# The gate of an encoder layer: from eight to seven block products, its weights prepared during the MLP, its sigmoid from one ScalarE function

## The chip, the cores and the metric

The kernel runs on one core of a Trainium2 chip. The core has five engines with queues of their own: TensorE (PE in the profile, with its weight loads as PEld), VectorE (DVE), ScalarE (ACT), GpSimd (POOL) and SyncE (SP), which here issues nearly all transfers. The metric is the device time of one execution in microseconds (us); less is better.

## The reference

One layer of an encoder runs over 1280 tokens (1024 and 256) of width 1024: an attention half, an MLP of width 4096 with squared ReLU, and then the part that is changed here, in 32-bit floats:

```python
gate = sigmoid(rms_norm(h, g_ple) @ w_ple_gate)      # (T, 1024) x (1024, 1024)
h = h + gate * (p @ w_ple_proj)                      # (T, 256) x (256, 1024)
y = rms_norm(h, g_final)
```

`rms_norm(h, g)` divides each row by the root of its mean square (plus 1e-6) and multiplies by the gains g.

## The kernel before

Every product of 32-bit operands is made from three products of a fast format: an operand a is split into a high part ah (a rounding copy on ScalarE) and a low part al = a - ah (a subtraction on VectorE or GpSimd), and PE adds ah·bh, ah·bl and al·bh into one PSUM bank (`split3`, L156 and L264). One matmul is 128x128 stationary by up to 512 moving columns.

The two MLP products are done as block products after Winograd's form of Strassen's scheme: both operands are cut into 2x2 blocks, and seven products of sums of blocks stand for the usual eight. The second MLP product goes through 56 steps m, eight for each of seven block products in the order O2 = 1, 7, 6, 4, 5, 3, 2. In step m `put2(m)` issues 30 matmuls, `prep(m + 3)` splits the operands of three steps later (a copy of 1280 columns and one of 1024 on ScalarE, L1384 and L1385, the same again as subtractions on VectorE, L1386 and L1387), and at its end `load2(m + 5)` asks for the operands of five steps later over SP's queue: 640 KB of activations from DRAM (`ar`) and none, one or two pieces of 512 KB of weights (`w2r`). The operand buffers rotate over three, so `prep(m + 3)` waits until `put2(m)` has been read. After a block's eighth step `evac2` adds the five PSUM banks to the residual h, which lies in four quadrants of 5 tiles x 512 columns (`hq`, by token half and column half).

The gate before is a plain product. From step 32 on `gate_w` loads rows of w_gate, multiplies them by g_ple and splits them, so that all eight 128-row pieces lie in SBUF; `gate_input(t)` transposes one token tile of h on PE (8 transposes, L1517), splits it (L1518, L1519) and makes the row scale rn = 1/rms from a squared sum, Ln and Exp with one correcting step (`rsqrt`, L138 to L144). Ten token tiles t then follow one another. For each of two column halves there are 24 gate matmuls (`psg`, L1588) and 6 of the embedding's product (`psp`, L156); the sigmoid is computed as exp(-ln(1 + exp(-z))) with a correction: ScalarE L1592, VectorE L1593, ScalarE L1594 and L1595, GpSimd L1596, VectorE L1597. The result multiplies the embedding (L1613), is added to h (GpSimd, L1615), is squared for the final norm (ScalarE, L1616), and VectorE applies row scale and gain (L1644) before the store. The last tile is cut into pieces of 512, 256 and 256 columns, and its arithmetic is on VectorE in place of GpSimd.

The order of the work on each engine comes from a scheduler that runs while the program is built: it walks the program with a simulated clock and gives each engine its instructions in that order; `issue_after(x)` forces what is in its block to come after x on x's engine. Each engine then works through its own queue in order. Tiles of one `slot` share one buffer, so a new tile waits until the last user of the old one is through.

Of the kernel before, what the change touches and what calls it, by code (L numbers as in the profile page):

```python
# [16 lines left out]
F16 = mybir.dt.float16  # L17
AF = mybir.ActivationFunctionType
# [5 lines left out]
P = 128  # L24
# [21 lines left out]
def encoder_kernel(ctx: ExitStack, tc: tile.TileContext, x, xT, pT, w_in, w_out, w_ff1, w_ff2, w_gate, w_proj,  # L46
# [88 lines left out]
    def rsqrt(dst, src, scale, eps, tp, n, tag):  # L135
        vv = tp.tile([P, n], F32, tag=f"{tag}v", name=f"{tag}v")
        uu = tp.tile([P, n], F32, tag=f"{tag}u", name=f"{tag}u")
        V.tensor_scalar(vv, src, scale, eps, op0=ALU.mult, op1=ALU.add)  # L138
        S.activation(uu, vv, AF.Ln)
        S.activation(dst, uu, AF.Exp, scale=-0.5)  # L140
        if n == 1:
            S.activation(uu, dst, AF.Copy, scale=-0.5)
            V.scalar_tensor_tensor(vv, dst, dst, vv, op0=ALU.mult, op1=ALU.mult)
            V.scalar_tensor_tensor(dst, vv, -3.0, uu, op0=ALU.add, op1=ALU.mult)  # L144
            return
# [3 lines left out]
        V.tensor_tensor(dst, dst, uu, op=ALU.mult)  # L149

# [57 lines left out]
    def open_slots(pool_, tags):  # L208
        for tag in tags:
            slot_pool[tag] = pool_  # L210
            size = {"H": 2560, "L": 2560, "W": 1024, "Q": 1280, "K": 1280, "T": 512}[tag[0]]
            slot(tag, [P, size], F32, tag)
# [1128 lines left out]
    open_slots(fq, ["Q2", "Q3"])  # L1341
# [8 lines left out]
    AOS, WOS, ARS, WRS = ("H0", "H2", "H3"), ("H1", "L7", "L5"), ("L1", "L6"), ("W8", "W9", "Q0", "Q1", "Q2", "Q3")  # L1350
# [3 lines left out]
    kt2 = {}  # L1354
    wr_n = itertools.count()
    w2v = w_ff2.rearrange("(b c x r) n -> b x r c n", c=2, x=2, r=P)

    def load2(m):
# [3 lines left out]
        t = AR[m] = slot(ARS[m % 2], [P, 2, HT], F32, "ar")  # L1362
        dma(t, ad[i][b].rearrange("c p t -> p c t"))
        WR[m] = []
        for x, y in WSRC[i]:
            if i == 1:
                t = kt2[b] = slot(KTS[b], [P, 2, 512], F32, "kt2")
            else:
                t = slot(WRS[next(wr_n) % 6], [P, 2, 512], F32, "w2r")
                WR[m].append(t[:])  # L1370
            dma(t, w2v[b, x][:, :, y * 512:y * 512 + 512])

    def prep(m):
# [13 lines left out]
        V.tensor_tensor(wo[:, 1], w, f(wo[:, 0]), op=ALU.subtract)  # L1387
# [13 lines left out]
    def load_h(half, n, tag):  # L1401
# [4 lines left out]
    BANKS = ("f2 pj f1 f2 tr", "pj tr f1 f2 pj", "f2 tr f1 pj tr", "f2 pj f1 f2 tr", "tr pj f1 f2 pj",  # L1406
             "f1 f2 tr tr pj", "f1 f2 pj f1 f2")
# [68 lines left out]
    FORD = [TORD[2 * j + h] for h in (1, 0) for j in range(HP)]  # L1476
    gw, pw, n3 = [], [], {}
    g_n = itertools.count()

    def w_raw(src):  # L1480
        n = next(g_n)
        t = slot("W10" if n < 4 else f"W{8 + n % 2}", [P, D], F32, "graw")
        dma(t, src)
        return t

    def gate_w(k, tags):
        raw = w_raw(w_gate[k * P:(k + 1) * P, :])
        if len(tags) == 1:
            t = at32(tags[0], [P, 2, D], F32R, "gw")
            a, b = t[:, 0], t[:, 1]  # L1490
        else:
            a, b = (slot(t, [P, D], F32R, "gw")[:] for t in tags)
        S.activation(a, raw, AF.Copy, scale=gple[:, k:k + 1])
        V.scalar_tensor_tensor(b, raw, gple[:, k:k + 1], f(a), op0=ALU.mult, op1=ALU.subtract)
        gw.append((a, b))

    def proj_w(k, tag):
        raw = w_raw(w_proj[k * P:(k + 1) * P, :])
        t = at32(tag, [P, 2, D], F32R, "pw")
        S.activation(t[:, 0], raw, AF.Copy)  # L1500
        V.tensor_tensor(t[:, 1], raw, f(t[:, 0]), op=ALU.subtract)
        pw.append((t[:, 0], t[:, 1]))

    gi_n = itertools.count()

    def h_half(t, n):
        j, half = divmod(TORD.index(t), 2)
        return h_of(j, half, n)

    def gate_input(t):  # L1510

        n3_ = at32(("H5", "L4")[next(gi_n) % 2], [P, 2, KD, P], F32R, "n3")
        n3h, n3l = n3_[:, 0], n3_[:, 1]
        for n in range(2):
            tr = pp2[0].tile([P, 4, P], F32, tag="tr", name="trg", bufs=2)
            for k in range(4):
                PE.transpose(tr[:, k], h_half(t, n)[:, k * P:(k + 1) * P], ident)  # L1517
            S.activation(n3h[:, 4 * n:4 * n + 4], tr, AF.Copy)  # L1518
            V.tensor_tensor(n3l[:, 4 * n:4 * n + 4], tr, f(n3h[:, 4 * n:4 * n + 4]), op=ALU.subtract)  # L1519
        ss = gq_.tile([P, 2], F32, tag="gss", name="gss")  # L1520
        for n in range(2):
            jk = gq_.tile([P, 512], F32, tag="gjk", name="gjk", bufs=1)
            S.activation(jk, h_half(t, n), AF.Square, accum_out=ss[:, n:n + 1])
        V.tensor_tensor(ss[:, 0:1], ss[:, 0:1], ss[:, 1:2], op=ALU.add)
        rn = gq_.tile([P, 1], F32, tag="grn", name="grn")
        rsqrt(rn, ss[:, 0:1], 1.0 / D, 1e-6, gq_, 1, "grs")
        S.activation(rn, rn, AF.Copy, scale=-1.0)
        return n3h, n3l, rn

    QUADS = {2: (0, 0, "H6"), 3: (0, 1, "L2"), 4: (1, 0, "H4"), 5: (1, 1, "L3")}  # L1530
    for m in range(NM):
# [3 lines left out]
        if m + 3 < NM:  # L1535
            prep(m + 3)

        if m >= 4 * NB and m % 4 == 0 and len(gw) < 4:
            gate_w(len(gw), KTS[2 * len(gw):2 * len(gw) + 2])
        if m == NM - 4:  # L1540
            fqs.close()
            gq_ = pool("gq", side="left", bufs=2)
            gq_.tile([P, 8], F32, name="gpad", bufs=1)
            for k in range(2):
                gate_w(4 + k, (ARS[k],))
        elif m == NM - 3:
            gate_w(6, (AOS[m % 3],))
            gate_w(7, (WOS[m % 3],))
            n3[FORD[0]] = gate_input(FORD[0])
# [147 lines left out]
```

## Time and profile before

| | us |
|---|---|
| median of 3 runs | 1693.11 (1692.22 to 1693.23) |
| profiled execution | 1691.84 |
| its span in the profile | 1690.1 |
| PE busy | 1651.6 |
| DVE busy | 1179.9 |
| ACT busy | 868.0 |
| POOL busy | 661.0 |
| the seven block products of the second MLP product | 1152 to 1535 |
| the gate, from its first matmul to the last of all | 1535 to 1679 |

The page of the profile lists busy time by engine, the span in 40 slices, the DMA queues, the chain of work that ended last, and the costliest groups of instructions; other views give the same for a stretch of time, for one line, or in order of time. "x24" is a count, and "<- PE" after an idle time names what ended it.

### The profile page before, as it was taken

The numbers are of one execution on the slowest core, as the hardware profiler recorded it, in microseconds if no ns is written. First come the engines' busy times: TensorE is split into PE (matmuls) and PEld (weight loads), VectorE is DVE, ScalarE is ACT, GpSimd is POOL, SyncE is SP. The second block draws the span as 40 slices with busy tenths as digits, with TensorE's granted clock in tenths as the row PEclk, the third lists the DMA queues.
The fourth block names the chain that finished last, engine by engine and source line by source line (L and its number), as shares of the span: only waits on it lengthen the run. The fifth ranks groups of instructions, "written<-read, shape, count | busy, mean of one in ns | idle before, by whom it ended". The sixth has DMA issues, their size and how long they took to land.

```text
span 1690.1 us, 27269 instructions
## 1 busy us (share of the span) xinstructions
PE 1651.6 (98%) x9849; PEld 1482.7 (88%) x9849; DVE 1179.9 (70%) x2119; ACT 868.0 (51%) x1749; POOL 661.0 (39%) x647
## 2 busy tenths in 40 slices
PE   8999999999899999999999999999999999999997
PEld 8999888888788888889999999998888888888886
DVE  7778588777888888668666666666665855445666
ACT  8643377776766667674333333233433333354554
POOL 1223455555654445433566665620532400001441
PEclk9999999999999999999999999999999999999999
DMA  9766843433954524395443343349676356532111
GB/s 309 239 216 237 247 144 110 133 108 98 273 161 130 154 74 131 108 330 172 160 136 131 132 159 128 135 169 386 220 225 203 124 192 210 177 117 75 35 44 50
DMA packets 191867, 278.28 MB, mean 165 GB/s; under 512 B 13674, under 2 KB 121076, under 8 KB 191732
## 3 DMA queue, kind: packets, MB, share of 16 engines
q1 hardware_dynamic: 189988, 271.28, 49.7%
q0 software_dynamic: 1600, 5.24, 1.0%
q8 instruction: 78, 1.28, 0.3%
q14 instruction: 57, 0.47, 0.1%
q10 hardware_dynamic: 144, 0.00, 0.0%
HBM read 182.63 MB, written 88.61 MB: 160 GB/s over the span
## 4 chain that ended last, share of the span: by engine, by line
PE 79%; DVE 8%; ACT 4%; issue 4%; POOL 2%; DMA 2%; POOLq 0%; SPq 0%; ACTq 0%; DVEq 0%
PE psa L264 6%; PE sc L651 6%; PE av L729 5%; PE psb L264 4%; PE pso L264 4%; PE tr L705 4%; PE psv L264 2%; PE psg L1588 1%; DVE pl L716 1%; DVE p L686 1%; DMA xt<-in_x 1%; POOL hq L1615 1%; DMA xr<-in_xT 1%; PE f__15605 L156 1%; PE f__16642 L156 1%
## 5 line engine op out<-in xcount | busy, mean ns | idle before, releaser
L1384 ACT ACTIVATE ao<-ar 128x1280 fp32r<-128x1280 f32 x56 | 71.2, 1273 | 183.7 <-PE f__15946 L156 36.6
L651 PE MATMUL sc<-kt,qt 128*128 128x512 f32 (+1 forms) x576 | 156.6, 392 | 8.8 <-ACT p L676 6.1
L716 DVE TENSOR_TENSOR pl<-tr,ph 128x512 fp32r<-128x512 f32 x204 | 138.0, 685 | 32.0 <-ACT ph L711 30.8
L1386 DVE TENSOR_TENSOR ao<-ar,ao 128x1280 fp32r<-128x1280 f32 x56 | 93.3, 1666 | 85.2 <-ACT ao L1384 85.2
L711 ACT ACTIVATE ph<-tr 128x512 fp32r<-128x512 f32 x204 | 120.0, 596 | 59.2 <-PE tr L705 52.7
L651 PEld LDWEIGHTS sc<-kt,qt 128*128 128x128 f32 x576 | 98.8, 189 | 27.1 <-ACT p L676 7.6
L264 PE MATMUL pso<-ow,mt 128*128 128x512 f32 x480 | 119.9, 396 | 2.0 <-DVE osq L756 1.3
L705 PE MATMUL tr<-ident,p 128*128 128x128 f32 x768 | 116.0, 274 | 5.8 <-DVE pl L716 5.1
L1588 PE MATMUL psg<-gw,n 128*128 128x512 f32 (+1 forms) x504 | 113.7, 381 | 0.0
L705 PEld LDWEIGHTS tr<-ident,p 128*128 128x128 f32 x768 | 91.6, 141 | 22.6 <-DVE pl L716 9.0
L1105 POOL TENSOR_SCALAR w1r<-w1r,gmlp 128x256 f32<-128x256 f32 x112 | 80.3, 735 | 68.4 <-DMA w1r<-in_w_ff 68.4
L1588 PEld LDWEIGHTS psg<-gw,n 128*128 128x128 f32 x504 | 90.9, 188 | 17.8
L264 PEld LDWEIGHTS pso<-ow,mt 128*128 128x128 f32 x480 | 88.0, 189 | 19.9 <-DVE osq L756 2.0
L729 PE MATMUL av<-ph,vt 128*128 128x256 f32 x544 | 101.8, 288 | 1.0 <-ACT ph L711 0.4
L690 POOL TENSOR_SCALAR p<-p,rl 128x1024 f32<-128x1024 f32 x64 | 76.2, 1192 | 50.6 <-DVE rl L688 49.1
L1178 ACT ACTIVATE w<-w1s 128x512 fp32r<-128x512 f32 x56 | 35.2, 629 | 114.7 <-POOL w1s L1185 55.3
L668 DVE TENSOR_REDUCE mm<-sc 128x1 f32<-128x1024 f32 (+1 forms) x80 | 84.2, 1056 | 9.4 <-PE sc L651 9.0
L729 PE MATMUL av<-pl,vt 128*128 128x256 f32 x408 | 89.4, 300 | 0.0
L729 PEld LDWEIGHTS av<-ph,vt 128*128 128x128 f32 x544 | 81.8, 188 | 6.4 <-DVE osq L756 0.8
L676 ACT ACTIVATE p<-sc,mm 128x1024 f32<-128x1024 f32 x64 | 71.4, 1116 | 25.1 <-DVE mm L668 16.3
L664 DVE CUSTOM_DVE_ANT_0 p<-sc,dist 128x1024 f32<-128x1024 f32 x64 | 77.6, 1218 | 7.8 <-PE sc L651 3.8
L673 ACT ACTIVATE p<-p,mm 128x1024 f32<-128x1024 f32 x64 | 73.5, 1149 | 18.0 <-DVE mm L664 17.2
(1520 smaller groups left out, 4705.9 us busy)
## 6 DMA issues: line engine op xcount, KB each, us to landing
ar<-ad SPq DMA_DIRECT2D x56, 640.0 KB, 4.0
w2r<-in_w_ff SPq DMA_DIRECT2D x56, 512.0 KB, 4.6
qt<-qd SPq DMA_DIRECT2D x160, 128.0 KB, 3.0
ad<-q SPq DMA_DIRECT2D x64, 320.0 KB, 2.8
ad<-qs SPq DMA_DIRECT2D x48, 320.0 KB, 2.2
w1r<-in_w_ff SPq DMA_DIRECT2D x28, 512.0 KB, 4.3
md<-ml SPq DMA_DIRECT2D x40, 256.0 KB, 2.5
mt<-md SPq DMA_DIRECT2D x20, 512.0 KB, 5.7
```

Source lines behind the costliest of these rows:

```text
L264: PE.matmul(ps, a, b, start=i == 0, stop=i == n - 1)
L651: PE.matmul(ps[:, h0:h0 + n], shared["q"][:, cc, v, i * P:(i + 1) * P], kt[:, s0 + h0:s0 + h0 + n], start=v == 0, stop=v == 1)
L664: V.tensor_tensor_reduce(out=p[:, :sn], in0=ps[:, :sn], in1=dst_t[:, off:off + sn], scale=SLOPES[idx], scalar=3.0e38, op0=ALU.add, op1=ALU ...
L668: V.tensor_reduce(out=st["m", i][:, 0:1], in_=ps[:, :sn], axis=AX.X, op=ALU.max, negate=True)
L690: G.tensor_scalar(p[:, :sn], p[:, :sn], rl[:, 0:1], 1.0, op0=ALU.mult, op1=ALU.mult)
L705: PE.transpose(t[:, jj, i * P:(i + 1) * P], st["ws"][i][:, j * P:(j + 1) * P], ident)
L711: S.activation(ph, st["tr", j2], AF.Copy)
L716: V.tensor_tensor(pl, st["tr", j2], f(st["ph", j2][:]), op=ALU.subtract)
L729: PE.matmul(st["av"][:, :256], x_, y_, start=j2 == 0 and n == 0, stop=j2 == nj - 1 and n == len(pr) - 1)
L1105: G.tensor_scalar(raw[:, k], raw[:, k], gmlp[:, 4 * kh + k:4 * kh + k + 1], 1.0, op0=ALU.mult, op1=ALU.mult)
L1386: V.tensor_tensor(ao[:, 1], a, f(ao[:, 0]), op=ALU.subtract)
L1588: ends[:] = [PE.matmul(ps, a, b, start=m == 0, stop=m == len(pr) - 1)]
```

## The change

The gate's product is done with the same seven block products (ORDER 1, 2, 6, 5, 3, 7, 4) on the quadrants of h and of g_ple·w_gate. Each has 5 token tiles x 4 x 3 matmuls. Sums of products are kept in two SBUF buffers m1 and u3; the products 2, 3, 7 and 4 finish one quadrant of the gate each, and only these have the embedding's product, the sigmoid and the addition to h (`gate_half`).

- **Weights.** In steps 29 to 43 of the MLP, a generator `gate_operands` takes one step after each `prep`: two loads of four quarters of w_gate scaled on ScalarE, five block operands each (sums on VectorE, none on GpSimd), split through one staging buffer (L6) and written to DRAM (`bed`); the last three steps split the embedding's input pT and write it too (`ped`). `b_ops` loads a block operand back one block ahead. Those of blocks 2 and 3 are raw quarters, loaded and split in place.
- **Tokens.** `quad_tr` transposes a quadrant when the MLP has finished it: quadrants 12, 11 and 21 in the MLP's last 24 steps, 22 in the gate's first block. `a_op` splits a block operand of tokens one block ahead; their sums are on GpSimd.
- **Sigmoid.** One ScalarE function with the row scale as its scale. This function is in another ScalarE table than Ln and Exp; the table of these is loaded again near the end.
- **Row scales.** `rsqrt_d` starts from an integer estimate of 1/sqrt and takes three Newton steps, on VectorE for the gate and on GpSimd for most final norms; the last two tiles of the output keep Ln and Exp.
- **Last tile.** Two pieces of 256 columns; the final scaling is split over VectorE and ScalarE, and the last store is issued by ScalarE.
- **Around it.** The two `ar` buffers lie in one slot, which frees L6; three instead of six `w2r` buffers from step 40 on; PSUM banks of the MLP's blocks five and six are renamed, which frees two for the transposes.

```diff
+    def rsqrt_d(dst, ss, tp, n, tag, eng=V, bufs=None, rest=None):
...
+        eng.tensor_scalar(vv, ss, -0.5 / D, c, op0=ALU.mult, op1=ALU.add)
+        eng.tensor_scalar(dst.bitcast(I32), vv[:].bitcast(I32), -0.5, float(0x5F3759DF - 2**30 - 2**22), op0=ALU.mult, op1=ALU.add)
+        for _ in range(3):
+            if n == 1:
+                eng.tensor_scalar(uu, dst, dst, vv, op0=ALU.mult, op1=ALU.mult)
+                eng.tensor_scalar(dst, uu, 1.5, dst, op0=ALU.add, op1=ALU.mult)
...
-        t = AR[m] = slot(ARS[m % 2], [P, 2, HT], F32, "ar")
-        dma(t, ad[i][b].rearrange("c p t -> p c t"))
+        if m == 0:
+            AR["both"] = slot("L1", [P, 2, 2, HT], F32, "ar")
+        t = AR[m] = AR["both"][:, m % 2]
+        fetched[:] = [dma(t, ad[i][b].rearrange("c p t -> p c t"))]
...
+    def a_op(i, j, src, eng=V):
...
+        S.activation(t[:, 0], src, AF.Copy)
+        eng.tensor_tensor(t[:, 1], src, f(t[:, 0]), op=ALU.subtract)
...
+    def gate_operands():
+        stage = slot("L6", [P, 2, 2, 512], F32R, "gbs")
+        def out(y, src, dst):
+            S.activation(stage[:, y, 0], src, AF.Copy)
+            V.tensor_tensor(stage[:, y, 1], src, f(stage[:, y, 0]), op=ALU.subtract)
+            dma(dst, f(stage[:, y]))
+        for x in range(2):
...
+            for t, k0, c0 in ((r11, 4, 0), (r22, 0, 512), (r12, 4, 512), (r21, 0, 0)):
+                k0 += 2 * x
+                dma(t, w_gate[k0 * P:(k0 + 2) * P, c0:c0 + 512].rearrange("(k p) c -> p k c", p=P))
+                for y in range(2):
+                    S.activation(t[:, y], t[:, y], AF.Copy, scale=gple[:, k0 + y:k0 + y + 1])
+            yield
+            for i, t, a, b, op in ((1, r11, None, None, None), (7, r22, r22, r12, ALU.subtract), (5, r12, r12, r11, ALU.subtract), (6, r11, r11, r22, ALU.add), (4, r21, r21, r11, ALU.subtract)):
+                if op is not None:
+                    V.tensor_tensor(t, a, b, op=op)
+                for y in range(2):
+                    out(y, t[:, y], bed[i][2 * x + y])
+                yield
...
     for m in range(NM):
         put2(m)
...
+        if m >= 29:
+            with tc.issue_after(fetched[0].ins), tc.issue_after(split[0].ins):
+                next(made, None)
...
-            S.activation(e, ps, AF.Exp, scale=rn)
-            V.tensor_scalar(d, e, 1e18, 1.0, op0=ALU.min, op1=ALU.add)
-            S.activation(e, d, AF.Ln)
-            S.activation(e, e, AF.Exp, scale=-1.0)
-            (V if late else G).tensor_tensor(d, d, e, op=ALU.mult)
-            V.scalar_tensor_tensor(e, d, -2.0, e, op0=ALU.add, op1=ALU.mult)
...
+    def gate_half(i, j):
...
+        if last:
+            es = []
+            for x in range(2):
+                ps, end = product(i, j, 256 * x, 256)
+                e = e_tile()[:, :256]
+                V.tensor_tensor(e, ps, acc_[:, 256 * x:256 * x + 256], op=ALU.add)
+                sig = S.activation(e, e, AF.Sigmoid, scale=rn)
+                es.append(e)
+            with tc.issue_after(sig.ins):
+                S.preload_act_table_set("natural_log_exp_and_others")
+            finish(half, j - 1)
...
+        ps, _ = product(i, j)
+        e = e_tile()
+        V.tensor_tensor(e, ps, acc_, op=ALU.add)
+        if i == 7:
+            V.tensor_tensor(m1[:, j], ps, m1[:, j], op=ALU.add)
+        S.activation(e, e, AF.Sigmoid, scale=rn)
+        combine(half, j, 512 * n, 512, e, embed(p, 512 * n, 512), n, e)
+        if i == 3 or i == 4 and j < 3:
+            finish(half, j)
...
+            if i == 1:
...
+                a_op(2, j, RA[12][:, j])
+                G.tensor_tensor(RA[12][:, j], RA[12][:, j], RA[11][:, j], op=ALU.add)
+                t = quad_tr(22, j)
+                S.activation(RA[22][:, j], t, AF.Copy)
+                V.tensor_tensor(RA["S1"][:, j], t, RA[21][:, j], op=ALU.add)
+                G.tensor_tensor(RA[21][:, j], RA[11][:, j], RA[21][:, j], op=ALU.subtract)
+                G.tensor_tensor(RA[11][:, j], RA["S1"][:, j], RA[11][:, j], op=ALU.subtract)
```

More of the change, by code (lines that the diff above doesn't have):

```diff
@@ L17 @@
 F16 = mybir.dt.float16
+I32 = mybir.dt.int32
 AF = mybir.ActivationFunctionType
@@ L137, in rsqrt @@
         uu = tp.tile([P, n], F32, tag=f"{tag}u", name=f"{tag}u")
-        V.tensor_scalar(vv, src, scale, eps, op0=ALU.mult, op1=ALU.add)
+        first = V.tensor_scalar(vv, src, scale, eps, op0=ALU.mult, op1=ALU.add)
         S.activation(uu, vv, AF.Ln)
@@ L1497, in proj_w @@
[L1497 to L1528, printed above, removed]
@@ L1531, in encoder_kernel @@
+    made = gate_operands()
+    raw21 = []
     for m in range(NM):
```

370 lines of the change are left out of this document (254 added, 116 removed).

## The prediction

> **What bounds the kernel now.** I read the page first, then the busy time of each engine in stretches, then the groups and the order of time of the gate, which is the last stage. The page:
>
> ```profile
> span 1690.1 us, 27269 instructions
> PE 1651.6 (98%) x9849; PEld 1482.7 (88%) x9849; DVE 1179.9 (70%) x2119; ACT 868.0 (51%) x1749; POOL 661.0 (39%) x647
> PEclk9999999999999999999999999999999999999999
> ```
>
> PE is busy 98% of the span at full clock. A busy PE could still be a waiting one, so I take its pace from the order of time. Columns: start, duration, engine, line, instruction, count.
>
> ```profile
> 1549.38 5.75 PE L1588 MATMUL psg<-gw,n 128*128 128x512 f32 x24
> 1548.59 1.03 PE L1517 MATMUL trg<-ident,hq 128*128 128x128 f32 x8
> 1556.33 5.60 PE L1588 MATMUL psg<-gw,n 128*128 128x512 f32 x24
> 1561.77 0.62 PE L156 MATMUL psp<-pw,p_h 128*128 128x512 f32 x2
> 1664.91 11.36 PE L1588 MATMUL psg<-gw,n 128*128 128x512 f32 x72
> 1678.80 0.28 PE L156 MATMUL psp<-pw,p_l 128*128 128x256 f32 x1
> ```
>
> 24 matmuls of 512 columns start at 1556.33 and the next group at 1561.77: 5.44/24 = 0.2267 us each. The last tile's 24 of 512 and 48 of 256 take 11.36, so one of 256 costs (11.36 - 5.44)/48 = 0.123. The last matmul ends at 1679.08, and 11.0 us follow it. The stretches of this stage and of the late second MLP product:
>
> ```profile
> 1535.10:1680.00 144.90, 143.98 (x695) 120.60 (x693) 90.91 (x167) 73.98 (x198) 48.77 (x40) 1.00 0.12 42
> 1349.30:1390.10 40.80, 40.80 (x181) 33.78 (x181) 23.31 (x22) 14.38 (x13) 0.00 (x0) 1.00 0.60 196
> 1390.10:1451.30 61.20, 61.20 (x271) 50.68 (x271) 32.94 (x31) 20.02 (x18) 0.00 (x0) 1.00 0.62 204
> 1141.00:1183.00 42.00, 42.00 (x216) 36.67 (x215) 25.84 (x32) 15.74 (x19) 2.41 (x1) 1.00 1.02 386
> ```
>
> Columns are PE, PEld, DVE, ACT, POOL busy, clock, DMA share, GB/s. From 1535.10 to 1679.08 PE is busy without a gap, and the list of PE's waits from 1150 on is empty. So the gate costs what its matmuls cost, and a matmul taken out there is worth its 0.2267 us, as long as the other engines keep up.
>
> **The matmuls.** The gate before is 10 token tiles x 2 column halves x 24 matmuls. These groups give the count:
>
> ```profile
> L1588 PE MATMUL psg<-gw,n 128*128 128x512 f32 x456 | 107.9, 392 | 0.0
> L1588 PE MATMUL psg<-gw,n 128*128 128x256 f32 x48 | 5.9, 283 | 0.0
> L1615 POOL TENSOR_TENSOR hq<-hq,ge 128x512 f32<-128x512 f32 x16 | 22.4, 1400 | 36.3 <-DVE ge L1613 36.3
> L1613 DVE TENSOR_TENSOR ge<-psp,ge 128x512 f32<-128x512 f32 x19 | 13.1, 691 | 1.2
> L1592 ACT ACTIVATE ge<-psg,grn 128x512 f32<-128x512 f32 x19 | 13.1, 689 | 25.2 <-PE psg L1588 25.2
> L143 DVE SCALAR_TENSOR_TENSOR grsv<-grn,grsv 128x1 f32<-128x1 f32 x8 | 10.0, 1251 | 0.0
> ```
>
> 456 x 0.2267 + 48 x 0.123 = 109.3 us. After: 7 products x 5 token tiles x 12 = 420, of which the last tile's 12 become 24 of 256: 408 x 0.2267 + 24 x 0.123 = 95.4. Gain 13.9. The embedding product keeps its 114 matmuls of 512 and 12 of 256, and the 80 transposes stay 80; 60 of them move ahead of the gate, which doesn't change PE's sum. They now come in fours. Around eight, the next 24 matmuls took 5.75 shown, 0.15 more than the 5.60 of an undisturbed group: 10 further seams cost 0 to 1.5 us, and I take 0.7.
>
> **The operands made in the late MLP.** Steps m = 29 to 43 last 30 x 0.2267 = 6.8 us each, 102 us in all (1349.3 to 1451.3). Added there on DVE: 8 sums and 3 pT splits of 1024 columns at 1.22 (row below) and 20 subtractions of 512 at 0.69: 27 us. With 56.3 there now and three gate weights leaving, about 80 of 102. ACT gets 16 scalings, 20 copies and 3 wide ones, some 25 us on 34. DMA is the tight one: 20 writes and 8 loads of 0.52 MB, pT in and out, 18.6 MB. Now 196 x 40.8 + 204 x 61.2 = 20.5 MB pass, of which 1.6 leave: 37.5 MB in 102 us, 368 GB/s. The stretch at 1141 moved 386 GB/s at share 1.02 with PE never idle. So the queue would be 95% full. The slack of one MLP operand:
>
> ```profile
> 1402.96 0.37 SPq L1363 DMA_DIRECT2D ar<-ad  x1
> ar<-ad SPq DMA_DIRECT2D x56, 640.0 KB, 4.0
> 1411.01 1.27 ACT L1384 ACTIVATE ao<-ar 128x1280 fp32r<-128x1280 f32 x1 [4.58 <-PE f__15946 L156]
> 1413.73 1.22 DVE L1387 TENSOR_TENSOR wo<-w2r,wo 128x1024 fp32r<-128x1024 f32 x1
> 1424.37 1.52 PE L156 MATMUL f__16300<-wo,ao 128*128 128x512 f32 x6
> ```
>
> The load is issued at 1402.96, lands 4.0 later, and ACT uses it at 1411.01 (it waited for PE to free the buffer, not for the load): 4.05 spare. DVE is done at 1414.95 and PE takes the operand at 1424.37: 9.42 spare. A step of operands stands in SP's queue between two such loads, ACT's copy waits until the single stage buffer L6 has been written out, and behind it waits the next `prep`; 13.5 us of delay can pass before PE notices. Cost taken: 0. If the cover went, the queue at 196/0.60 = 327 GB/s would need 115 us, 13 late, which is just the slack; lower bound 0, upper 6.
>
> **The elementwise work of the gate.** Removed per half tile: Exp, Ln, Exp on ACT, the capped +1, POOL's product and one scalar-tensor-tensor on DVE; added: one PSUM add and the sigmoid. Per block of five token tiles, with DVE at 0.69 for 512 columns and 1.41 for the two final scalings (row in the next fences): first block (PE 13.6 + 2.2 for transposes) 23 DVE instructions, 15.9 us; second (PE 20.4) 13.8; fifth (PE 20.4) 5 x (4 x 0.69 + 1.41) = 20.9; the others between half and nine tenths of PE's time. ACT never has over 19 us in 20.4. The weights come back from HBM by four loads of 0.52 MB for each of five blocks, on SP's queue beside the stores of y; that is 10.5 MB more in a stage that moves 42 GB/s now, each set is asked for a whole block (13.6 us) ahead, and it costs nothing unless it lands that late. So DVE is level with PE in blocks one and five. POOL gets three adds for each tile in block one, and that hurts DVE:
>
> ```profile
> 1313.94 16.08 POOL L1428 TENSOR_TENSOR hq<-hq,acc 128x512 f32<-128x512 f32 x8 [0.63 <-DVE acc L1428]
> 1318.95 3.48 DVE L1428 TENSOR_TENSOR acc<-acc 128x512 f32<-128x512 f32 x2
> 1324.06 2.58 DVE L1386 TENSOR_TENSOR ao<-ar,ao 128x1280 fp32r<-128x1280 f32 x1
> 1337.73 1.48 DVE L1386 TENSOR_TENSOR ao<-ar,ao 128x1280 fp32r<-128x1280 f32 x1
> 1684.85 0.22 DVE L143 SCALAR_TENSOR_TENSOR rfv<-rf,rfv 128x1 f32<-128x1 f32 x1 [0.51 <-ACT rf L140]
> ```
>
> While POOL runs, a DVE instruction with both inputs in SBUF takes up to 1.1 us longer (2.58 against 1.48; L143's single column 1.25 against 0.22), and POOL's adds take 2.01 instead of 1.40. In block one 13 of DVE's 23 have two SBUF inputs: 0 to 14 us more; I take the middle, 7. DVE then ends block one 7 us after PE. PE's cover: six PSUM banks of products, and two for the embedding. The third embedding of block two starts 2 x 4.08 + 2.72 = 10.9 after the block's start and needs the first bank back, so 7 us late plus 2 of arithmetic still fits. Stalls over the gate: 0 to 8, I take 2. The Newton steps on POOL (9 instructions of one column, no such row; below the 0.74 that POOL's 256 columns take now) lie beside PE and only delay stores; taken at 0 on the path, their wait is part of the 2.
>
> **The end.** Before, from the last matmul to the end 11.0 us pass:
>
> ```profile
> 1682.33 0.42 DVE L1613 TENSOR_TENSOR ge<-psp,ge 128x256 f32<-128x256 f32 x1
> 1683.24 0.42 ACT L1616 ACTIVATE ge<-hq 128x256 f32<-128x256 f32 x1 [0.29 <-DVE hq L1615]
> 1685.18 0.16 DVE L144 SCALAR_TENSOR_TENSOR rf<-rfv,rfu 128x1 f32<-128x1 f32 x1
> 1675.21 1.41 DVE L1644 SCALAR_TENSOR_TENSOR hq<-hq,rf,gfin 128x512 f32<-128x512 f32 x2
> 1686.58 0.46 SPq L1640 DMA_DIRECT2D y<-hq  x1
> L115 ACT ACT_TABLE_LOAD x1 | 1.3, 1283 | 0.7 <-PEq L1688 0.7
> ```
>
> The last product by the embedding starts 3.25 us after PE's end, because the gate's arithmetic is still running. After, the last gate needs an add (0.42) and a sigmoid (0.46) beside 12 embedding matmuls (1.4), so it can start 0.1 after. That gives 3.15. Against it stand a table load, 1.28 by the row of the only one there is, and the previous tile's row scale and two final scalings (1.41) on the same engines. I take back 1.15: gain 2.0, bounds +3.2 and -0.1. The first sigmoid's load lies in block two beside matmuls. "ScalarE: Activation LUTs" in the Trainium skill, section What ACT_TABLE_LOAD costs, speaks against this change: a switch of sets costs 2.66 us, a drain with the load. By that page the gain of the end would be 0.6 and the time 1681.4 instead of 1680.0; the trace, whose one load comes before any work, can show no drain.
>
> **Sum.** Against the profiled execution (1691.84, of which 1690.1 is the span and 1.7 lies around it): -13.9 + 0.7 + 0 + 2 - 2.0 = -13.2, span 1676.9, execution 1678.6. The median of the runs shown, 1693.11, is 1.3 above that execution: 1693.1 - 13.2 = 1680, rounded.
>
> **The rivals.** (1) DVE and POOL bind the gate. Worst case of block one, 14 us late, less 4 of cover, plus block five, where the final scaling waits for POOL's row scale in DVE's order, 3 to 4 beyond its cover, less the 6.6 that block two wins back: stall 8 instead of 2, time 1686. For it: the 1.1 us above; against: DVE has a quarter to a half of blocks two to four free. "GPSIMD Engine Reference" in the Trainium skill, section Key points, speaks for it too: GpSimd shares its SBUF interfaces with VectorE and collides with instructions of two SBUF inputs; the trace agrees, 2.58 against 1.48.
> (2) Nothing gained. The chain of waits, in order of time, has pieces such as these:
>
> ```profile
> 1630.62 1.42 POOL hq L1615
> 1675.21 1.41 DVE hq L1644 x2
> 1676.62 0.60 DVE gd L1596
> ```
>
> The end hangs on DVE, ACT and POOL from 1563 on, not on PE, so it could come as late without those matmuls. Then the matmuls' gain shows as PE idle and only what I count for the end is left: 1693.1 - 2.0 = 1691. Against: DVE has 90.9 busy of 144.9.
> (3) Slower: late MLP transfers. New writes and their reads through one queue, the p writes in 512-byte pieces. PE starves when delay exceeds 13.5 us; the loss is 37.5 MB/R - 102 - 13.5, and it eats the whole gain of 13.2 below R = 292 GB/s. At 270 it is 23.4: 1703. For: no cover left at 327 GB/s; against: 386 shown with this kind of transfer.
>
> **Chances.** Forecast 0.62 (own range 1675.5 to 1685), rival 1 0.20 (1683 to 1690), rival 2 0.07, rival 3 0.11. The lowest case is all gains and no stall, -13.9 - 3.2 = 1676, less half a microsecond of scatter. Range 1675.5 to 1690.5 leaves out rival 3, most of 2 and a little of the rest. A difference of 0.2% (3.4 us) is what a measurement can tell: faster means below 1689.7. Forecast and nearly all of rival 1: 0.82; same 0.08; slower 0.10.
>
> **What would show it.** Right: 432 gate matmuls in place of 504, PE without gaps from 1150 to its end at about 1667, DMA share near 0.95 in steps 29 to 43, some 9 us after the last matmul, two more table loads. Wrong: PE waiting on `ao` or `wo` after 1349 (rival 3), PE waiting on DVE in blocks two or six (rival 1), more than 11 us after the last matmul (the table load with a drain), gate matmuls spaced wider than 0.2267, or more than two further table loads.

## The result, and the profile after

The changed kernel takes 1682.18 us (median of 4 runs, 1681.1 to 1684.48); the kernel before, measured beside it, takes 1692.66 (1692.18 to 1693.23). The ratio is 0.9944, with a 95% interval of 0.9932 to 0.9957: 10.5 us gained where 13.1 were forecast. The profiled execution took 1681.64. From its page:

```profile
span 1679.9 us, 27290 instructions
PE 1639.0 (98%) x9777; PEld 1469.5 (87%) x9777; DVE 1202.9 (72%) x2130; ACT 879.3 (52%) x1716; POOL 664.2 (40%) x697
PEclk9999999999999999999999999999999999999998
```

PE has 12.6 us less work and the span is 10.2 shorter. Where the two differ is read from the stretches. Columns: start and end, length, PE, PEld, DVE, ACT, POOL busy with instruction counts, clock, DMA share, GB/s. The second MLP product and the gate of the kernel before:

```profile
1152.00:1535.10 383.10, 383.10 (x1700) 317.12 (x1699) 227.47 (x193) 148.82 (x173) 72.17 (x32) 1.00 0.60 198
1535.10:1679.08 143.98, 143.98 (x695) 120.60 (x693) 89.99 (x165) 73.50 (x196) 48.77 (x40) 1.00 0.12 43
```

The same two of the changed kernel, what follows its last matmul, and a stretch of MLP steps in which the operands are made:

```profile
1150.90:1540.30 389.40, 388.76 (x1740) 321.11 (x1741) 245.39 (x228) 178.59 (x225) 75.20 (x34) 1.00 0.69 240
1540.32:1667.08 126.76, 126.64 (x579) 104.06 (x577) 94.62 (x138) 55.23 (x109) 47.73 (x81) 1.00 0.44 150
1667.08:1679.90 12.82, 0.00 (x0) 0.00 (x0) 7.38 (x22) 5.28 (x17) 2.87 (x8) 0.65 0.33 124
1390.10:1451.30 61.20, 61.20 (x283) 50.67 (x282) 48.83 (x62) 41.70 (x65) 0.00 (x0) 1.00 0.94 341
```

| us | before | after | difference |
|---|---|---|---|
| start of the second MLP product | 1152.1 | 1151.0 | -1.1 |
| second MLP product | 382.9 | 389.4 | +6.5 |
| gate, first to last matmul | 144.1 | 126.8 | -17.4 |
| after the last matmul | 11.0 | 12.8 | +1.8 |
| span | 1690.1 | 1679.9 | -10.2 |

(The gate's first matmul starts at 1534.96 before, 0.14 ahead of the stretch above.) In the runs of the changed kernel and its variants, which are alike up to the first row, this start lay between 1149.8 and 1155.2, so the -1.1 is taken as scatter. 64 transposes stood in the gate before and 20 stand there now: 44 moved into the MLP at some 0.117 each, 5.2 us. That is most of the +6.5, and the gate is lighter by as much. The list of PE's waits from 1100 to 1680 holds two entries (total, times, longest), of which the second lies just ahead of the second MLP product:

```profile
PE f__15611 L176 <- DVE wo L1412: 0.6, 1, 0.6
PE f__14582 L176 <- DVE q L1322: 0.2, 1, 0.2
```

The first of them begins at 1328.2, ahead of the steps in which the operands are made. In the gate this list shows no wait. PE's groups there, by shape (count, then busy time and mean ns):

```profile
L1696 PE MATMUL psg<-gbo,gao 128*128 128x512 f32 x363 | 88.0, 392 | 0.0
L176 PE MATMUL psp<-pw,p_hl 128*128 128x512 f32 x114 | 29.0, 395 | 0.0
L1696 PE MATMUL psg<-gao 128*128 128x512 f32 x45 | 13.0, 393 | 0.0
L1509 PE MATMUL trg<-ident,hq 128*128 128x128 f32 x20 | 3.2, 275 | 0.1
L1696 PE MATMUL psg<-gbo,gao 128*128 128x256 f32 x24 | 3.2, 283 | 0.0
```

363 + 45 + 24 are the 432 gate matmuls. At the durations of the prediction they cost 95.4, the embedding's 27.3, and 20 transposes in fours (0.36 + 0.11 each four) 2.35: 125.1. Measured are 126.76. The 1.7 between is seen in the order of time (start, duration, engine, instruction, count):

```profile
1577.42 13.80 PE L1696 MATMUL psg<-gbo,gao 128*128 128x512 f32 x60
1591.06 0.84 PE L1696 MATMUL psg<-gao 128*128 128x512 f32 x3
...
1608.78 2.93 PE L1696 MATMUL psg<-gbo,gao 128*128 128x512 f32 x12
1611.55 1.56 PE L176 MATMUL psp<-pw,p_hl 128*128 128x512 f32 x6
1612.95 3.15 PE L1696 MATMUL psg<-gbo,gao 128*128 128x512 f32 x13
```

60 gate matmuls in one piece start 13.64 ahead of what follows (60 x 0.2267 is 13.60). 12 followed by the embedding's product take 2.77 instead of 2.72, and those 6 take 1.40 instead of 1.36. Most switches between the two products cost 0.04 to 0.05 us; there are 31, and by the order of time they come to about 1.0. Some 0.3 more lies around the last four transposes, at the start of block two: from 1555.84 to 1557.30 pass 1.46, where three matmuls and four transposes cost 1.15. The rest is spread in hundredths.

The end, in order of time. After the last matmul (1667.08), with what ended an idle time in brackets:

```profile
1667.74 0.47 DVE L1681 TENSOR_TENSOR hq<-hq,ge 128x256 f32<-128x256 f32 x1
1667.77 0.49 ACT L1752 ACTIVATE ge<-ge,grn 128x256 f32<-128x256 f32 x1
1668.28 1.28 ACT L1755 ACT_TABLE_LOAD   x1
1668.30 0.42 DVE L1679 TENSOR_TENSOR ge<-psp,ge 128x256 f32<-128x256 f32 x1
1668.76 0.42 DVE L1681 TENSOR_TENSOR hq<-hq,ge 128x256 f32<-128x256 f32 x1
1669.58 0.42 ACT L1682 ACTIVATE ge<-hq 128x256 f32<-128x256 f32 x1
1670.08 0.40 ACT L1682 ACTIVATE ge<-hq 128x256 f32<-128x256 f32 x1
1670.39 0.19 ACT L1682 ACTIVATION_READ_ACCUMULATOR ge<-hq 128x1 f32 x1
1670.67 1.42 DVE L1733 SCALAR_TENSOR_TENSOR hq<-hq,rf,gfin 128x512 f32<-128x512 f32 x2 [0.89 <-POOL rf L165]
1672.83 0.21 DVE L139 TENSOR_SCALAR rfzv<-fss,rc 128x1 f32<-128x1 f32 x1
1673.28 1.41 DVE L1733 SCALAR_TENSOR_TENSOR hq<-hq,rf,gfin 128x512 f32<-128x512 f32 x2
1674.94 0.21 DVE L144 SCALAR_TENSOR_TENSOR rfzv<-rf,rfzv 128x1 f32<-128x1 f32 x1
1675.27 0.16 DVE L145 SCALAR_TENSOR_TENSOR rf<-rfzv,rfzu 128x1 f32<-128x1 f32 x1
```

L1679 is VectorE's product by the embedding, L1681 the addition to h (on VectorE now for every tile), L1682 the square and its sum. From the kernel before, the end of the last squared sum and the first step of the last row scale:

```profile
1683.57 0.19 ACT L1616 ACTIVATION_READ_ACCUMULATOR ge<-hq 128x1 f32 x1
1684.20 0.15 DVE L138 TENSOR_SCALAR rfv<-fss 128x1 f32<-128x1 f32 x1
```

The last product by the embedding starts 1.2 after the last matmul, against 3.25 before: 2.0 gained. But from its start to the last row scale 7.1 pass (1668.30 to 1675.43), against 3.0 before (1682.33 to 1685.34): 4.1 lost. Of these 0.8 lie before the last squared sum ends (1670.58): the table load holds the first square back by 1.3, and behind it the last one starts 0.9 after its input is there. 1.8 more pass from that sum to L139, because VectorE works in order and first scales an earlier tile; 1.5 go to the next tile's scaling, which stands ahead of L144. VectorE comes to L139 2.25 after the sum is there, so by this trace the table load wasn't what L139 waited for. And the first of these scalings was itself late: VectorE waited 0.89 for GpSimd's Newton steps. Over the gate VectorE waited for those (waits from 1540 on: total, times, longest):

```profile
DVE hq L1733 <- POOL rf L165: 6.0, 7, 2.2
```

So the theory for the experiments: the gate is bound by PE alone, making the operands costs nothing, and the end is set by VectorE's order with the wait for GpSimd's row scales in it. The rivals: the making or the transfers bind the MLP; VectorE and GpSimd bind the gate; the table load sets the end.

### The profile page after: what moved, and what is told of

It is laid out like the page before. It is cut to its first block, busy times and chain, and to the rows that moved or that the text cites. A ratio compares the mean times of both kernels' runs of the same rounds, so it can differ in the third digit from the quotient of the medians.

```text
span 1679.9 us, 27290 instructions
## 1 busy us (share of the span) xinstructions
PE 1639.0 (98%) x9777; PEld 1469.5 (87%) x9777; DVE 1202.9 (72%) x2130; ACT 879.3 (52%) x1716; POOL 664.2 (40%) x697
## 5 line engine op out<-in xcount | busy, mean ns | idle before, releaser
L1696 PE MATMUL psg<-gbo,gao 128*128 128x512 f32 (+1 forms) x387 | 91.0, 385 | 0.0
L1801 POOL TENSOR_TENSOR ra<-ra 128x512 f32<-128x512 f32 x5 | 7.1, 1429 | 204.9 <-DVE gao L1542 204.9
L1696 PEld LDWEIGHTS psg<-gbo,gao 128*128 128x128 f32 x387 | 70.9, 188 | 14.7
```

What stands on the lines that cost most here:

```text
L1696: ends[:] = [PE.matmul(ps, a, w, start=n == 0, stop=n == len(pr) - 1)]
```

## The experiments

Times are medians. The kernel before, on the chip of each group of runs, took 1692.48, 1693.65 and 1691.44. "Gate" is the time from the first matmul of its products to the last matmul, "end" what follows to the end of the span. Profiled executions of the variants differ by up to 6 us ahead of the gate, mostly in work that no edit touches, so gate and end are compared, and whole times by the ratios.

| run | us | ratio to before, 95% | gate | end |
|---|---|---|---|---|
| changed kernel | 1682.18 | 0.9944 (0.9932 to 0.9957) | 126.8 | 12.8 |
| d1_twice | 1696.54 | 1.0023 (1.0013 to 1.0034) | 140.4 | 12.8 |
| d2_unmade | 1683.00 | 0.9937 (0.9922 to 0.9951) | 126.7 | 12.4 |
| d3_three | 1661.61 | 0.9814 (0.9794 to 0.9834) | 104.9 | 14.8 |
| d4_nopool | 1680.68 | 0.9928 (0.9912 to 0.9945) | 126.4 | 12.5 |
| t0_control | 1684.77 | 0.9948 (0.9934 to 0.9963) | 126.8 | 12.8 |
| t1_newton_dve | 1681.64 | 0.9927 (0.9911 to 0.9943) | 126.8 | 11.8 |
| t2_no_reload | 1684.91 | 0.9949 (0.9935 to 0.9964) | 126.8 | 13.9 |
| t3_both | 1685.91 | 0.9953 (0.9938 to 0.9968) | 126.8 | 13.8 |
| u1_order | 1681.11 | 0.9939 (0.9927 to 0.9951) | 128.6 | 10.2 |
| u2_order_newton | 1684.48 | 0.9954 (0.9942 to 0.9966) | 128.7 | 10.9 |
| u5_chain | 1684.38 | 0.9959 (0.9947 to 0.9971) | 128.6 | 12.3 |
| s1_old_sigmoid | 1710.10 | 1.0111 (1.0097 to 1.0125) | 154.2 | 12.9 |

**An eighth product.** Block 6 is multiplied twice, 60 matmuls more that nothing needs.

```diff
+                if i == 6:
+                    product(i, j)
                 ps, _ = product(i, j)
```

> The changed kernel with the sixth block product issued twice (60 more matmuls of 512 columns; the second result is read, the first is thrown away). Theory (the gate is bound by PE, the end by its own chain): PE's end and the execution move by 60 x 0.2267 = +13.6 us, to about 1695.8, and what follows the last matmul stays at about 12.8. Rival (the elementwise engines set the gate's pace and PE fills in): part of it is hidden, +0 to +7, 1682 to 1689.

The gate of this kernel, in stretches:

```profile
1544.76:1685.11 140.35, 140.24 (x639) 115.41 (x637) 94.78 (x138) 55.23 (x109) 47.74 (x81) 1.00 0.41 135
```

It is 13.59 longer, and 60 x 0.2267 is 13.60; PE has no wait in it. Each matmul of the gate is on the path with its full price, and that is what the 13.9 of the seven products rest on. With as many gate matmuls as the kernel before (480 of 512 columns or their equal), the new arrangement is 4.1 us slower than it, so the rest of the change, taken together, brings no gain of its own.

**The operands not made.** Only block 1's operand is prepared, split and written. The sums, splits and writes for blocks 7, 5, 6 and 4 fall away, and these blocks load block 1's operand in place of their own; the loads of w_gate stay.

```diff
-                if op is not None:
+                if op is None:
+                    pass
+                if False:
                     V.tensor_tensor(t, a, b, op=op)
                 for y in range(2):
-                    out(y, t[:, y], bed[i][2 * x + y])
+                    if i == 1:
+                        out(y, t[:, y], bed[i][2 * x + y])
...
-                dma(f(t[:]), bed[i][k])
+                dma(f(t[:]), bed[1][k])
```

> The changed kernel with four of the five prepared weight operands left out: no sums on VectorE, no splits and no writes for blocks 7, 5, 6 and 4 (16 of 20 writes of 0.52 MB), which load block 1's operand instead, so y is not the reference's. Theory (late operands lie beside PE): the DMA share between 1390 and 1451 falls from 0.94 to about 0.7, the time moves by 0 to -1.5 us, 1680.7 to 1682.2. Rival (the transfers or VectorE's added work delay the MLP): -3 us or more, 1679 or less.

A stretch in which the operands were made:

```profile
1390.10:1451.30 61.20, 61.20 (x283) 50.75 (x282) 37.34 (x48) 37.90 (x56) 0.00 (x0) 1.00 0.77 267
```

VectorE is 11.5 us lighter and the DMA share falls from 0.94 to 0.77, but the second MLP product takes 389.27 against 389.36. Making these four operands cost PE nothing that can be told from scatter (0.9 between runs with the same MLP, see t0_control below): it is hidden, at a queue 94% full. The wait of 0.6 for `wo` is in this run too, so it doesn't come from these four either.

**A quarter of the gate's matmuls left out.**

```diff
-        for k in range(4):
+        for k in range(3):
```

> The changed kernel with three of four k pieces in every block product (a quarter of the gate's matmuls left out, so y is not the reference's): 102 matmuls of 512 and 6 of 256 columns fewer, 23.9 us of PE. Theory (PE bound with room on the other engines): -20 to -24 us, 1658 to 1662, with PE's first waits on DVE in the blocks with the embedding. Rival (DVE and GpSimd are level with PE, as rival 1 of the prediction had it): -10 us or less, 1672 or more.

```profile
PE psp L176 <- DVE ge L1679: 0.8, 1, 0.8
PE psp L176 <- DVE hq L1681: 0.3, 1, 0.3
```

These are all of PE's waits in the gate of this kernel. It took 104.94, so 21.8 of the 23.9 us of matmuls left out were gained there, and only then do the other engines begin to show; the end is 2.0 longer, as more of their work is left behind the last matmul. VectorE and GpSimd let the gate shrink by some 20 us: they don't bind the gate of the changed kernel.

**GpSimd's sums left out.** The four token sums in blocks one and two are dropped, which takes away what VectorE collides with.

```diff
-                G.tensor_tensor(RA[12][:, j], RA[12][:, j], RA[11][:, j], op=ALU.add)
...
-                G.tensor_tensor(RA[21][:, j], RA[11][:, j], RA[21][:, j], op=ALU.subtract)
-                G.tensor_tensor(RA[11][:, j], RA["S1"][:, j], RA[11][:, j], op=ALU.subtract)
...
-                    G.tensor_tensor(RA[12][:, j], RA[12][:, j], RA["S1"][:, j], op=ALU.subtract)
```

> The changed kernel without the 20 additions on GpSimd in the gate's first two blocks (sums of token quadrants left out, so y is not the reference's). Theory (VectorE's collisions with GpSimd there are covered by PE): DVE's instructions with two SBUF inputs fall from about 1.2 us to their undisturbed duration in the first 35 us of the gate, the time moves by 0 to -0.5 us, about 1682. Rival (they cost PE time): -2 us or more, 1680 or less.

Two groups of VectorE between 1535 and 1600, first of the changed kernel, then of this one (busy us, mean ns, idle before):

```profile
L1659 DVE TENSOR_TENSOR pw<-gr,pw 128x512 fp32r<-128x512 f32 x1 | 1.6, 1620 | 0.3 <-ACT pw L1658 0.3
L161 DVE TENSOR_SCALAR grn<-grsv 128x5 int32<-128x5 int32 x1 | 1.2, 1218 | 0.0
```

```profile
L1659 DVE TENSOR_TENSOR pw<-gr,pw 128x512 fp32r<-128x512 f32 x1 | 0.7, 692 | 0.1
L161 DVE TENSOR_SCALAR grn<-grsv 128x5 int32<-128x5 int32 x1 | 0.2, 170 | 0.0
```

The collisions are real, 0.93 and 1.05 us for one instruction here, and over the whole gate VectorE's busy time falls from 94.6 to 84.4. The gate is only 0.4 shorter, and 0.3 of that is the stretch around the last four transposes, which has its undisturbed length here: the stall that rival 1 put at 8 and the forecast at 2 was 0.4.

**The row scales at the end on VectorE.** First the changed kernel again, to see the scatter:

> The changed kernel once more, beside the three that follow, as their measure: about 1682.2 us, 12.8 us from the end of the last matmul to the end of the span.

It has the same gate and end to 0.1 us, at 1684.77. Its second MLP product, without any wait of PE, takes 388.5, and so does that of d4_nopool: the 389.4 above hold 0.9 of scatter. Now the last quadrant's Newton steps move from GpSimd to VectorE:

```diff
-            rsqrt_d(rf[:], ss[:, half:half + 1], gq_, 1, "rf", G, 4, rest=ss[:, 1 - half:2 - half])
+            rsqrt_d(rf[:], ss[:, half:half + 1], gq_, 1, "rf", G if half else V, 4, rest=ss[:, 1 - half:2 - half])
```

> The changed kernel with the Newton steps of the last quadrant's first three tiles on VectorE in place of GpSimd (9 instructions of one column each). Theory A (the end is late because VectorE, in order, holds final scalings that wait for GpSimd's Newton steps): the waits on rf go, what follows the last matmul falls from 12.8 to 10 or 11, the time by 2 to 3 us. Rival B (the end hangs on ScalarE's table load between the last sigmoid and the last squares): no change, within 0.5. Rival C (VectorE simply has too much to do at the end): 4.5 us more work on VectorE, no gain or a loss up to 1.

The end in order of time; the last matmul ended at 1670.63:

```profile
1673.58 0.19 ACT L1682 ACTIVATION_READ_ACCUMULATOR ge<-hq 128x1 f32 x1
1674.02 2.73 DVE L1733 SCALAR_TENSOR_TENSOR hq<-hq,rf,gfin 128x512 f32<-128x512 f32 x4
1676.67 0.21 DVE L139 TENSOR_SCALAR rfzv<-fss,rc 128x1 f32<-128x1 f32 x1
```

At the end VectorE no longer waits for GpSimd, and this end is 1.0 shorter, at 11.8; the theory had 10 to 11. What stands ahead of the last row scale is now four scalings in one piece, 2.73 us: the squared sums are there at 1673.77 and L139 comes at 1676.67. So GpSimd's steps were a part; the rest stands in VectorE's own queue.

**No table load at the end.** The last two tiles use Newton steps on VectorE in place of Ln and Exp, and the reload of the table goes.

```diff
-            first = rsqrt(rf, ss[:, 2:3], 1.0 / D, c, gq_, 1, "rfz")
+            first = rsqrt_d(rf[:], ss[:, 2:3], gq_, 1, "rfz", V, rest=c)
...
-            rsqrt(rf, ss[:, 0:1], 1.0 / D, 1e-6, gq_, 1, "rfw")
+            rsqrt_d(rf[:], ss[:, 0:1], gq_, 1, "rfw", V, rest=ss[:, 1:2])
...
-            with tc.issue_after(sig.ins):
-                S.preload_act_table_set("natural_log_exp_and_others")
```

> The changed kernel with the last two tiles' row scales by Newton steps on VectorE, so that Ln, Exp and the second table load go; the others stay on GpSimd. Theory A: the load is hidden behind VectorE's waits, 0 to -1 us, 12 to 13 after the last matmul. Rival B: -1.3 us by the load's row. The Trainium skill's page ScalarE: Activation LUTs (What ACT_TABLE_LOAD costs) has 2.66 us for a switch with its drain: by that, an estimate of up to -2.7.

The end is 13.9, 1.1 longer, with no load in it. The load isn't what makes the end long, as the 2.25 above had it too: the chain of Newton steps that replaces Ln and Exp in VectorE's queue costs more than leaving out the load's 1.28 saves. Both edits together:

> Both: all row scales of the last quadrant by Newton steps on VectorE, no second table load. Theory A: the two gains add up once the waits on GpSimd are gone, 9 to 10.5 us after the last matmul, -2.5 to -4 us. Rival C: no better than the kernel as it is.

13.8. This missed the expectation: on VectorE a Newton step is two single-column instructions (0.27 and 0.21) that wait for one another, some 0.56 for a step, and scalings stand between them.

**The order on PE.** In the changed kernel the embedding products of two tiles often come together (12 matmuls at 1652.28 and 1659.98, after 22 gate matmuls each), so VectorE gets two tiles at once, late. Here each block product comes after the embedding of the tile before:

```diff
-        split3(pq, pr)
+        for n_, (a, b) in enumerate(pr):
+            emb[:] = [PE.matmul(pq, a, b, start=n_ == 0, stop=n_ == len(pr) - 1)]
...
-        for n, (a, w) in enumerate(pr):
-            ends[:] = [PE.matmul(ps, a, w, start=n == 0, stop=n == len(pr) - 1)]
+        with tc.issue_after(emb[0].ins) if emb else contextlib.nullcontext():
+            for n, (a, w) in enumerate(pr):
+                ends[:] = [PE.matmul(ps, a, w, start=n == 0, stop=n == len(pr) - 1)]
```

> The changed kernel with PE's order in the gate forced: each tile's embedding product stands before the next tile's block product, where the scheduler had put the embeddings of two tiles together in the blocks 7 and 4. Theory D (the end is late because VectorE gets two tiles at once, late, and so carries a backlog past PE's end): 10.5 to 11.5 us after the last matmul in place of 12.8, -1.5 to -2.5 us, and still waits on GpSimd's rf. Rival C (VectorE has too much work in the last block whatever the order): 12.5 to 13, no change. Rival E (the order was needed: PE now waits for the embedding's banks): +1 us or more, with waits of PE on DVE.

PE's one wait in this gate, the same wait in u2_order_newton below, and then the stretch of u1_order after its last matmul:

```profile
PE psp L1674 <- DVE hq L1683: 1.3, 1, 1.3
```

```profile
PE psp L1674 <- DMA p_hl<-ped: 1.5, 1, 1.5
```

```profile
1673.65:1683.80 10.15, 0.00 (x0) 0.00 (x0) 5.68 (x20) 4.56 (x14) 0.00 (x0) 0.62 0.42 155
```

The end is 2.6 shorter: GpSimd is through before the last matmul, and L139 starts 0.03 after the last squared sum is there (2.25 in the changed kernel). But the gate is 1.8 longer, as much as rival E had it, though not for its reason. The first list names VectorE for the wait, but the embedding's bank had long been read: PE goes on at 1638.61, and the product that read that bank ended at 1632.65. What came then was the embedding's input `p_hl`: its load was issued at 1631.02, behind four weight loads of 512 KB and two stores, and took 7.5 to land, until 1638.5; in u2_order_newton the list names this load itself. Net 0.8, and the ratio (0.9939) can't be told from the changed kernel's 0.9944. With the Newton steps on VectorE as well:

> The forced order, and the Newton steps of the last quadrant's first three tiles on VectorE in place of GpSimd (which alone gave 11.8 us after the last matmul). Theory D: without the backlog and without waits on GpSimd, 9.5 to 10.5 after the last matmul, -2.5 to -3.5 us against the changed kernel. Rival C: 11.5 to 12, as with the Newton steps alone.

Gate 128.7 (the wait for `p_hl` is 1.5) and end 10.9: nothing is won over u1_order or the changed kernel. Last, VectorE's order at the end is written out by hand: tile 3's first scaling, then the last tile's pieces, and tile 3's second scaling after the last tile's own.

```diff
-            finish(half, j - 1)
...
+            first3 = scaled(0)
...
+                with tc.issue_after(first3.ins):
+                    combine(half, j, 256 * x, 256, es[x], pq, 2 * x, e_tile()[:, :256])
+            done = finish(half, j, True)
+            with tc.issue_after(done.ins):
+                scaled(1)
```

> As the one before, and VectorE's order at the end written out: the last but one tile's row scale by Newton steps on VectorE and half of its final scaling before the last tile's arithmetic, the other half behind all; only the last tile uses Ln and Exp. Theory D: the last squares end 2.5 to 3.5 us after the last matmul and nothing stands between them and the last row scale, 8.5 to 9.5 us after the last matmul, -3.5 to -4.5 us against the changed kernel, about 1678. Rival B (the table load holds the last squares): over 10.

The end is 12.3, a miss. The two scalings of tile 2, the Newton steps of tile 3 and its first scaling stand ahead of the last tile's pieces, and these start only at 1673.54, 3.5 after the last matmul. The order that I wrote put work in front of the last chain instead of behind it.

**The old sigmoid under the seven products.** Exp, the capped +1, Ln, Exp, GpSimd's product and the correction return in place of the one function; memory leaves five `ge` buffers instead of six and one `gd` buffer (the kernel before had two).

```diff
+    def old_gate(e, ps, a, rn, n, eng):
+        d = gq_.tile([P, 512], F32, tag="gd", name="gd", bufs=1)[:, :n]
+        V.scalar_tensor_tensor(e, ps, -1.0, a, op0=ALU.mult, op1=ALU.subtract)
+        S.activation(e, e, AF.Exp, scale=rn)
+        V.tensor_scalar(d, e, 1e18, 1.0, op0=ALU.min, op1=ALU.add)
+        S.activation(e, d, AF.Ln)
+        S.activation(e, e, AF.Exp, scale=-1.0)
+        eng.tensor_tensor(d, d, e, op=ALU.mult)
+        V.scalar_tensor_tensor(e, d, -2.0, e, op0=ALU.add, op1=ALU.mult)
...
-        V.tensor_tensor(e, ps, acc_, op=ALU.add)
+        old_gate(e, ps, acc_, rn, 512, V if i == 4 and j > 2 else G)
...
-        S.activation(e, e, AF.Sigmoid, scale=rn)
```

> The changed kernel with its sigmoid undone: per half tile the old Exp, cap and 1 added, Ln, Exp, product (GpSimd) and correction in place of one ScalarE function, no other function table (one buffer fewer for its results). Theory (matmuls give the gain, the sigmoid the room for it on VectorE): 5 x 1.1 us more on VectorE in each of the four blocks with the embedding, level with or above PE's 20.6; PE gets waits of 1 to 4 us and the end 13 to 16 us after the last matmul: +2 to +7 us. Rival (the one function gives no room that is needed, and its two table loads cost what it saves): within 1 us of the changed kernel.

The waits from 1640 on, and then two stretches late in its gate:

```profile
ACT ge L1741 <- DVE gd L1740: 24.4, 10, 4.3
...
PE psp L176 <- DVE ge L1679: 20.1, 7, 4.0
DVE ge L1744 <- POOL gd L1743: 9.5, 7, 1.9
```

```profile
1655.00:1680.00 25.00, 14.00 (x57) 9.89 (x56) 13.94 (x25) 12.35 (x25) 7.08 (x10) 0.84 0.18 52
1680.00:1695.00 15.00, 5.63 (x18) 3.93 (x18) 10.48 (x18) 4.50 (x10) 11.82 (x23) 0.61 0.25 88
```

and the capped +1 of three half tiles and a late embedding product in order of time:

```profile
1666.07 0.42 DVE L1740 TENSOR_SCALAR gd<-ge 128x512 f32<-128x512 f32 x1
1671.20 0.42 DVE L1740 TENSOR_SCALAR gd<-ge 128x512 f32<-128x512 f32 x1
1676.32 0.42 DVE L1740 TENSOR_SCALAR gd<-ge 128x512 f32<-128x512 f32 x1
1682.01 2.93 PE L176 MATMUL psp<-pw,p_hl 128*128 128x512 f32 x6 [2.62 <-DVE ge L1679]
```

Its gate is 27.4 us longer, and it is slower than the kernel before; the expectation was far too low. In the first of these stretches no engine is full: VectorE is busy 13.94 of 25. By the order of time the pace there is that of one half tile's round trip through VectorE, ScalarE, GpSimd and VectorE again: it repeats every 5.1 us, while PE's matmuls for a half tile take 4.16 in the changed kernel, and each L1740 comes after the correction that frees the single `gd` buffer. Over a longer stretch, from 1612.76 to 1688.17, the embedding products of the half tiles come 5.8 apart on average (13 intervals, 4.16 would make 54 of these 75 us): some 21 of the 27.4. For the earlier part, where VectorE is busy 12.36 of 15 (1640 to 1655), the round trip isn't shown to be the limit. So with this form of the sigmoid, in the memory left for it here, the gain of the seven products is more than lost. Whether a second `gd` buffer would let the round trips overlap wasn't tried; how much of the loss is due to the single buffer stays open.

## Why the prediction was right or wrong

**Time and direction.** 1682.18 against 1680, within the range and within the forecast's own narrower one; faster, as forecast. The sum was -13.2 for the span; the trace has -10.2.

**The matmuls: right.** -13.9 was the term (-13.84 unrounded); d1_twice measures 13.59 for 60 matmuls against 13.60 worked out. 432 matmuls are there, and the list of PE's waits shows none in the gate. The spacing marker failed slightly: the gate holds 1.65 beyond its matmuls and transposes, 1.0 of it at the seams between product and embedding, which the prediction didn't have. It charged 0.7 for transposes in fours; a group of four costs 0.36 + 0.11 and so half of a group of eight (0.94), and only the last group has 0.3 more. 44 transposes moved ahead of the gate, not 60: the kernel before had 16 of its 80 there already.

**The operands in the late MLP: right in cost, late in time.** The DMA share is 0.94 from 1390 to 1451 against a forecast 0.95, and d2_unmade shows no cost beyond scatter. Rival 3 fell with it. But the work came later than the prediction placed it: the first operand is written at 1372.1, the stretch from 1349.3 to 1390.1 has a share of 0.61, and the dense one goes from 1380 to 1500 (0.96, 345 GB/s, PE busy throughout) in place of 1349 to 1451. The second MLP product is 1.3 longer than its moved transposes explain; t0_control and d4_nopool put 0.9 of that to scatter (0.6 is the wait for `wo`, ahead of the making), and 0.4 stay unexplained.

**The stalls of the gate: 2 taken, 0.4 measured.** The collisions that the prediction took from the adds in the MLP came as it said: by d4_nopool they cost VectorE 10.2 us over the gate, where it took 7 for block one, and the gate 0.4. No wait of PE for a bank of products or embeddings is in the list, so the cover was enough. Rival 1 fell. Rival 2 fell too: d1_twice and d3_three move the end with the matmuls.

**The end: wrong, and the sign too.** Forecast -2.0, measured +1.8; this 3.8 is more than the whole miss. "so it can start 0.1 after" was measured as 1.2. The step that failed behind it is "I take back 1.15": of the table load and one tile's scalings, 2.69 by its rows, it left more than half beside the path, and in its place 4.1 were lost between the start of the last product by the embedding and the last row scale. VectorE works in order, and two pairs of scalings stood ahead of the two instructions that the last row scale needs. The sentence that took GpSimd's Newton steps "at 0 on the path" failed with it: t1_newton_dve gives them 1.0 of the end, and u1_order, where tiles reach VectorE in an even order, takes 2.6 off. Of "more than 11 us after the last matmul (the table load with a drain)" only the number came true: t2_no_reload has no load and is longer. "ScalarE: Activation LUTs" in the Trainium skill, section What ACT_TABLE_LOAD costs, gives 2.66 us for a switch with its drain; here the load starts 0.02 after the sigmoid ends, takes 1.28, and the next square starts 0.02 after it, so on this trace the switch cost 1.28 and no drain is seen.

**The account.** -13.84 matmuls, +1.65 seams and last transposes, +1.32 in the MLP (0.9 of it scatter), +1.80 end, -1.13 scatter ahead of the MLP product: -10.20.

**Still open.** How to have u1_order's end without its longer gate, which would be worth some 2.6 us; 1.3 of the gate's 1.8 is the wait for `p_hl`, and asking for `p_hl` earlier, ahead of the weight loads, wasn't tried. No variant that computes y beats the changed kernel by more than its interval: t1_newton_dve and u1_order have the lowest ratios of these, and the intervals overlap. Why a switch between products costs 0.04 us wasn't tried.

## What to carry to other kernels

In a stage where PE has neither gap nor wait, count matmuls and multiply: that came within 2 us in 127, and an extra copy of a product is a cheap way to prove it. For what follows the last matmul, write down each engine's queue in order and look at what stands ahead of the instructions of the last chain; side work such as an earlier tile's scaling costs its full length there, and a tiny step given to another engine blocks an in-order engine that waits for it. A change of arithmetic with many hops between engines is priced by its round trip and its buffers, not by busy time.

## What the runs showed of the hardware

A table load amid work cost ScalarE its 1.28 us, with 0.02 on either side of it. GpSimd's arithmetic on a single column mostly takes 0.19 to 0.34 us an instruction, now and then 0.5 to 1.2, and a row scale of eight of them, each waiting for the last, took 3.7 (1666.95 to 1670.63) and up to 4.5 (1658.39 to 1662.85, beside another). An elementwise instruction of 128 x 5 on VectorE with a single tensor input took 1.22 us beside GpSimd's sums and 0.17 without (L161 above), so the delay isn't proportional to size. In s1_old_sigmoid the granted clock fell to 0.84 and 0.61 where PE paused again and again, and six embedding matmuls that take 1.56 in the changed kernel took 2.93: waits of PE cost more than their own length there. A load of 256 KB that stood behind four of 512 KB and two stores took 7.5 us to land in u1_order, against 2.8 for the one issued just ahead of them.
